# Log-softmax backward on one core: unequal pieces of y, and the next group's first piece queued ahead of each store

## The chip, the cores and the metric

The kernel runs on one NeuronCore of a Trainium2 chip, the other cores idle. The metric is device time in microseconds (us); lower is better. Three runs of the kernel before, taken ahead of everything else, gave a median of 1867.34 us (1867.21 to 1867.37). The span in a profile is about 1.9 us shorter than the time (1865.4 against 1867.34 for the kernel before).

## The reference

```python
batch, seq_len, vocab = 8, 1024, 8192            # float32, 8192 rows of 8192
def reference(y, dy):
    softmax_x = np.exp(y)
    sum_dy = np.sum(dy, axis=-1, keepdims=True)
    return (dy - softmax_x * sum_dy).astype(np.float32)
```

Two tensors of 268.4 MB are read and one of 268.4 MB is written: 805.3 MB in all. The arithmetic needs the row sum of dy, one exponential per element, and one multiply-add per element.

## The kernel before

A group is 256 rows, two neighbouring rows on each of 128 partitions, so a group's dy, y and output are tiles of 128 x 16384 columns; there are 32 groups. dy has two buffers and is overwritten in place by the result. y has two half-size buffers of 8192 columns and is overwritten in place by its exponential.

```python
    R = 2; CD = D // 2
    dyp = ctx.enter_context(tc.tile_pool(name="dyp", bufs=2))
    yp = ctx.enter_context(tc.tile_pool(name="yp", bufs=R))

    def load_dy(g):                       # one transfer, then minus the row sums
        dy_t = dyp.tile([P, R * D], fp32, name="dy_t")
        nc.sync.dma_start(out=dy_t[:], in_=dy_v[g])
        ...                               # nc.vector.tensor_reduce(..., op=ALU.add, negate=True)

    def compute(dy_t, s_t, y_ts):         # four pieces of 4096 columns
        for r in range(R):
            for c in range(0, D, CD):
                e = y_ts[r][:, c : c + CD]
                d = dy_t[:, r * D + c : r * D + c + CD]
                nc.scalar.activation(e, e, EXP)
                nc.vector.scalar_tensor_tensor(out=d, in0=e, scalar=s_t[:, r : r + 1],
                                               in1=d, op0=ALU.mult, op1=ALU.add)
    cur = load_dy(0)
    for g in range(G):
        ...                               # the last two groups are cut here
        y_ts = load_y(g)                  # two transfers of 8192 columns
        compute(*cur, y_ts)
        nxt = load_dy(g + 1)
        store(g, cur[0])
        cur = nxt
```

All transfers are issued from SyncE's queue, in program order: y, y, dy of the next group, store, and again. A transfer that has to wait holds up those behind it. The store waits for the last multiply-add of its group. The dy load waits for the store before it, whose buffer it takes.

Of the kernel before, what the change touches and what calls it, by code (L numbers as in the profile page):

```python
# [1 line left out]

# [5 lines left out]


EXP = mybir.ActivationFunctionType.Exp  # L10
ALU = mybir.AluOpType


@with_exitstack
def kernel(
    ctx: ExitStack,
    tc: tile.TileContext,
    y: bass.AP,
    dy: bass.AP,
    out: bass.AP,  # L20
):



    nc = tc.nc
    P = nc.NUM_PARTITIONS
    fp32 = mybir.dt.float32

    N, D = y.flatten_outer_dims().shape
    R = 2  # L30
    G = N // (P * R)
    assert N == G * P * R
    CD = D // 2

    y_v = y.flatten_outer_dims().rearrange("(g p r) d -> g p (r d)", p=P, r=R)
    dy_v = dy.flatten_outer_dims().rearrange("(g p r) d -> g p (r d)", p=P, r=R)
    out_v = out.flatten_outer_dims().rearrange("(g p r) d -> g p (r d)", p=P, r=R)

    dyp = ctx.enter_context(tc.tile_pool(name="dyp", bufs=2))
    yp = ctx.enter_context(tc.tile_pool(name="yp", bufs=R))  # L40
    stats = ctx.enter_context(tc.tile_pool(name="stats", bufs=2))

    def load_dy(g):
        dy_t = dyp.tile([P, R * D], fp32, name="dy_t")
        nc.sync.dma_start(out=dy_t[:], in_=dy_v[g])
        s_t = stats.tile([P, R], fp32, name="s_t")
        nc.vector.tensor_reduce(  # L47
            out=s_t[:],
            in_=dy_t[:].rearrange("p (r d) -> p r d", r=R),
            axis=mybir.AxisListType.X,  # L50
            op=ALU.add,
            negate=True,
        )
        return dy_t, s_t

    def load_y(g):
        y_ts = []
        for r in range(R):
            y_t = yp.tile([P, D], fp32, name="y_t")
            nc.sync.dma_start(out=y_t[:], in_=y_v[g][:, r * D : (r + 1) * D])  # L60
            y_ts.append(y_t)
        return y_ts

    def compute(dy_t, s_t, y_ts):
        for r in range(R):
            for c in range(0, D, CD):
                e = y_ts[r][:, c : c + CD]
                d = dy_t[:, r * D + c : r * D + c + CD]
                nc.scalar.activation(e, e, EXP)  # L69
                nc.vector.scalar_tensor_tensor(  # L70
                    out=d, in0=e, scalar=s_t[:, r : r + 1], in1=d, op0=ALU.mult, op1=ALU.add
                )

    def store(g, dy_t, parts=1):
        w = R * D // parts
        for k in range(parts):
            nc.sync.dma_start(  # L77
                out=out_v[g][:, k * w : (k + 1) * w], in_=dy_t[:, k * w : (k + 1) * w]
            )

    cur = load_dy(0)
    for g in range(G):
        if g < G - 1:
            y_ts = load_y(g)
            compute(*cur, y_ts)
            nxt = load_dy(g + 1)
            if g < G - 2:
                store(g, cur[0])
                cur = nxt
            else:  # L90
                held, cur = cur, nxt
        else:
            y_ts = load_y(g)
            compute(*cur, y_ts)
            store(g - 1, held[0])
            store(g, cur[0], parts=R)


# [1 line left out]
_INS = ['y', 'dy']  # L100
_OUTS = [((8, 1024, 8192), 'float32')]


# [23 lines left out]
```

## Time and profile before

First the page of the kernel before: busy time by engine (microseconds, share of the span, instructions), the row of the transfer engines in 40 slices (tenths), what they moved in each slice, and the transfer queue (packets, MB, share of 16 engines' span).

```profile
DVE 1119.2 (60%) x160; ACT 457.1 (25%) x129; POOL 0.2 (0%) x4
...
DMA  9999999999999999999999999999999999999999
GB/s 427 416 434 431 443 433 422 435 437 436 427 433 431 440 430 434 431 429 441 433 437 425 433 442 431 434 425 436 438 434 433 428 434 437 437 431 430 429 435 396
...
q1 hardware_dynamic: 18576, 805.31, 99.9%
```

VectorE (DVE) is busy 60%, ScalarE (ACT) 25%, and the 16 transfer engines 99.9%. Moving bytes is the limit. Next is one steady group, near the end of the run, in the timeline of the kernel before (start, duration, engine, line, operation, tile; in brackets the idle time before it and what ended it; SPq is SyncE's queue):

```profile
1741.77 0.34 SPq L77 DMA_DIRECT2D out_dram<-dy_t  x1
1742.21 0.85 SPq L60 DMA_DIRECT2D y_t<-in_y_dram  x2
1748.49 17.22 DVE L47 TENSOR_REDUCE s_t<-dy_t 128x2 f32<-128x16384 f32 x1 [6.75 <-DMA dy_t<-in_dy_dram]
1767.83 0.33 SPq L45 DMA_DIRECT2D dy_t<-in_dy_dram  x1
...
1787.27 7.12 ACT L69 ACTIVATE y_t<-y_t 128x4096 f32<-128x4096 f32 x2 [2.58 <-DMA y_t<-in_y_dram]
```

Read it as a queue. The store is issued at 1741.77. The dy load ahead of it lands at 1748.49, when the reduction that waited for it starts. So 1748.49 - 1741.77 = 6.7 us of work was still queued when the store joined. This is called the reserve at the store here. Likewise the dy load is issued at 1767.83 while y lands until 1787.27: a reserve of 19.4 us. The idea to be tested is that the arithmetic can't cost time as long as no reserve runs out.

The start of the kernel before is tighter:

```profile
22.74 17.22 DVE L47 TENSOR_REDUCE s_t<-dy_t 128x2 f32<-128x16384 f32 x1 [22.74 <-DMA dy_t<-in_dy_dram]
...
57.77 0.35 SPq L77 DMA_DIRECT2D out_dram<-dy_t  x1
58.21 0.92 SPq L60 DMA_DIRECT2D y_t<-in_y_dram  x2
61.83 17.22 DVE L47 TENSOR_REDUCE s_t<-dy_t 128x2 f32<-128x16384 f32 x1 [4.09 <-DMA dy_t<-in_dy_dram]
```

There the reserve is 61.83 - 57.77 = 4.1 us. And the waits of SyncE's queue (total us, times, longest us): SyncE spends its time waiting for the multiply-add (L70) and for stores to land, which is harmless while the engines behind it have work.

```profile
SPq L77 <- DVE dy_t L70: 985.9, 32, 35.0
SPq L45 <- DMA out_dram<-dy_t: 742.0, 30, 25.6
```

| Read from the kernel before | value |
|---|---|
| steady group, reduction start to reduction start | 58.07 us for 25.17 MB, 433.4 GB/s |
| one packet of 65,536 bytes, one of 32,768 bytes (trace records, medians) | 2.418 us, 1.213 us |
| 805.31 MB at 65,536 bytes per 2.418 us on 16 engines (estimate) | 1857 us |

The Trainium skill ("DMA: Bandwidth & Descriptors", "Where 436 GB/s comes from") puts the ceiling of the fabric at 435 GB/s; this trace agrees, with 433.4 GB/s in a steady group.

### The profile page before, as it was taken

The numbers are of one execution on the slowest core, as the hardware profiler recorded it, in microseconds if no ns is written. First come the engines' busy times: TensorE is split into PE (matmuls) and PEld (weight loads), VectorE is DVE, ScalarE is ACT, GpSimd is POOL, SyncE is SP. The second block draws the span as 40 slices with busy tenths as digits, with TensorE's granted clock in tenths as the row PEclk, the third lists the DMA queues.
The fourth block names the chain that finished last, engine by engine and source line by source line (L and its number), as shares of the span: only waits on it lengthen the run. The fifth ranks groups of instructions, "written<-read, shape, count | busy, mean of one in ns | idle before, by whom it ended". The sixth has DMA issues, their size and how long they took to land.

```text
span 1865.4 us, 712 instructions
## 1 busy us (share of the span) xinstructions
DVE 1119.2 (60%) x160; ACT 457.1 (25%) x129; POOL 0.2 (0%) x4
## 2 busy tenths in 40 slices
DVE  5675555755557555575555755657656576565664
ACT  2123321233212332123321233212332113331132
POOL 0000000000000000000000000000000000000000
DMA  9999999999999999999999999999999999999999
GB/s 427 416 434 431 443 433 422 435 437 436 427 433 431 440 430 434 431 429 441 433 437 425 433 442 431 434 425 436 438 434 433 428 434 437 437 431 430 429 435 396
DMA packets 18582, 805.36 MB, mean 432 GB/s; under 512 B 2064, under 2 KB 2064, under 8 KB 2064
## 3 DMA queue, kind: packets, MB, share of 16 engines
q1 hardware_dynamic: 18576, 805.31, 99.9%
q14 instruction: 6, 0.05, 0.0%
HBM read 536.87 MB, written 268.44 MB: 432 GB/s over the span
## 4 chain that ended last, share of the span: by engine, by line
DMA 74%; DVE 17%; ACT 6%; SPq 1%; issue 1%; DVEq 0%; ACTq 0%
DMA y_t<-in_y_dram 69%; DVE dy_t L70 15%; ACT y_t L69 6%; DMA dy_t<-in_dy_dram 3%; DVE s_t L47 2%; DMA out_dram<-dy_t 1%; SPq L60 1%; SPq L77 1%; DVEq L122 0%; ACTq L69 0%; DVEq L70 0%
## 5 line engine op out<-in xcount | busy, mean ns | idle before, releaser
L70 DVE SCALAR_TENSOR_TENSOR dy_t<-y_t,s_t,dy_t 128x4096 f32<-128x4096 f32 x128 | 568.1, 4481 | 490.3 <-ACT y_t L69 490.1
L69 ACT ACTIVATE y_t<-y_t 128x4096 f32<-128x4096 f32 x128 | 455.9, 3608 | 1375.6 <-DMA y_t<-in_y_dram 1375.6
L47 DVE TENSOR_REDUCE s_t<-dy_t 128x2 f32<-128x16384 f32 x32 | 551.0, 17220 | 232.1 <-DMA dy_t<-in_dy_dram 232.1
L69 ACT ACT_TABLE_LOAD x1 | 1.3, 1283 | 0.7 <-PEq L111 0.7
L111 POOL MEMSET const-bfloat16-1.0<- 128x1 bf16 x1 | 0.1, 102 | 0.0
L111 POOL MEMSET const-uint8-127<- 128x1 uint8 x1 | 0.1, 102 | 0.0
L111 POOL MEMSET const-float32-1.0<- 128x1 f32 x1 | 0.1, 99 | 0.0
L111 POOL MEMSET const-float32-0.0<- 128x1 f32 x1 | 0.1, 98 | 0.2 <-issue 0.2
## 6 DMA issues: line engine op xcount, KB each, us to landing
y_t<-in_y_dram SPq DMA_DIRECT2D x64, 4096.0 KB, 35.9
out_dram<-dy_t SPq DMA_DIRECT2D x2, 4096.0 KB, 22.6
dy_t<-in_dy_dram SPq DMA_DIRECT2D x32, 38.7
out_dram<-dy_t SPq DMA_DIRECT2D x31, 26.1
```

The lines of the kernel that those rows point to most:

```text
L47: nc.vector.tensor_reduce(out=s_t[:], in_=dy_t[:].rearrange("p (r d) -> p r d", r=R), axis=mybir.AxisListType.X, op=ALU.add, negate=True,)
L60: nc.sync.dma_start(out=y_t[:], in_=y_v[g][:, r * D : (r + 1) * D])
L69: nc.scalar.activation(e, e, EXP)
L70: nc.vector.scalar_tensor_tensor(out=d, in0=e, scalar=s_t[:, r : r + 1], in1=d, op0=ALU.mult, op1=ALU.add)
L77: nc.sync.dma_start(out=out_v[g][:, k * w : (k + 1) * w], in_=dy_t[:, k * w : (k + 1) * w])
L111: nc = _bacc.Bacc("TRN2", target_bir_lowering=False, num_devices=1)
```

## The change

The intent is to balance the two reserves. y of a group comes as one piece of 5120 and one of 11264 columns. The first piece of the next group goes into the queue ahead of the store, so that more is queued when the store waits for arithmetic; less is then queued when the dy load waits for the store. The arithmetic goes in six pieces, small ones first after the second y piece. The first dy comes by rows, so the first reduction can start sooner. The main lines of the change (left out are, among others, the split first load of dy and a third buffer for the row sums):

```diff
-    CD = D // 2
+    A = 5120
+    A_PIECES = [(0, A)]
+    B_PIECES = [(5120, 6144), (6144, 8192), (8192, 10240), (10240, 13312), (13312, 16384)]
-    yp = ctx.enter_context(tc.tile_pool(name="yp", bufs=R))
+    yap = ctx.enter_context(tc.tile_pool(name="yap", bufs=1))
+    ybp = ctx.enter_context(tc.tile_pool(name="ybp", bufs=1))
...
-    cur = load_dy(0)
-    for g in range(G):
-        ...
+    def first_piece(g, x):
+        compute(*x, load_y(yap, g, 0, A, "ya_t"), 0, A_PIECES)
+    def second_piece(g, x):
+        compute(*x, load_y(ybp, g, A, W, "yb_t"), A, B_PIECES)
+    cur = load_dy(0, split=True)
+    first_piece(0, cur)
+    for g in range(G - 1):
+        second_piece(g, cur)
+        nxt = load_dy(g + 1)
+        first_piece(g + 1, nxt)
+        if g == G - 2:
+            second_piece(g + 1, nxt)
+        nc.sync.dma_start(out=out_v[g], in_=cur[0][:])
+        cur = nxt
+    for c in range(0, W, D):
+        nc.sync.dma_start(out=out_v[G - 1][:, c : c + D], in_=cur[0][:, c : c + D])
```

More of the change, by code (lines that the diff above doesn't have):

```diff
@@ L30 @@
     R = 2
+    W = R * D
     G = N // (P * R)
-    assert N == G * P * R
-    CD = D // 2
+    assert N == G * P * R and D == 8192
+    A = 5120
+    A_PIECES = [(0, A)]
+    B_PIECES = [(5120, 6144), (6144, 8192), (8192, 10240), (10240, 13312), (13312, 16384)]
     y_v = y.flatten_outer_dims().rearrange("(g p r) d -> g p (r d)", p=P, r=R)
@@ L39 @@
     dyp = ctx.enter_context(tc.tile_pool(name="dyp", bufs=2))
-    yp = ctx.enter_context(tc.tile_pool(name="yp", bufs=R))
-    stats = ctx.enter_context(tc.tile_pool(name="stats", bufs=2))
-    def load_dy(g):
-        dy_t = dyp.tile([P, R * D], fp32, name="dy_t")
-        nc.sync.dma_start(out=dy_t[:], in_=dy_v[g])
-        s_t = stats.tile([P, R], fp32, name="s_t")
-        nc.vector.tensor_reduce(
-            out=s_t[:],
-            in_=dy_t[:].rearrange("p (r d) -> p r d", r=R),
-            axis=mybir.AxisListType.X,
-            op=ALU.add,
-            negate=True,
-        )
-        return dy_t, s_t
@@ L56, in load_y @@
-    def load_y(g):
-        y_ts = []
-        for r in range(R):
-            y_t = yp.tile([P, D], fp32, name="y_t")
-            nc.sync.dma_start(out=y_t[:], in_=y_v[g][:, r * D : (r + 1) * D])
-            y_ts.append(y_t)
-        return y_ts
-    def compute(dy_t, s_t, y_ts):
-        for r in range(R):
-            for c in range(0, D, CD):
-                e = y_ts[r][:, c : c + CD]
-                d = dy_t[:, r * D + c : r * D + c + CD]
-                nc.scalar.activation(e, e, EXP)
-                nc.vector.scalar_tensor_tensor(
-                    out=d, in0=e, scalar=s_t[:, r : r + 1], in1=d, op0=ALU.mult, op1=ALU.add
-                )
@@ L74, in store @@
-    def store(g, dy_t, parts=1):
-        w = R * D // parts
-        for k in range(parts):
-            nc.sync.dma_start(
-                out=out_v[g][:, k * w : (k + 1) * w], in_=dy_t[:, k * w : (k + 1) * w]
-            )
-    cur = load_dy(0)
-    for g in range(G):
-        if g < G - 1:
-            y_ts = load_y(g)
-            compute(*cur, y_ts)
-            nxt = load_dy(g + 1)
-            if g < G - 2:
-                store(g, cur[0])
-                cur = nxt
-            else:
-                held, cur = cur, nxt
-        else:
-            y_ts = load_y(g)
-            compute(*cur, y_ts)
-            store(g - 1, held[0])
-            store(g, cur[0], parts=R)
+    yap = ctx.enter_context(tc.tile_pool(name="yap", bufs=1))
@@ new lines, with load_dy @@
+    ybp = ctx.enter_context(tc.tile_pool(name="ybp", bufs=1))
+    stats = ctx.enter_context(tc.tile_pool(name="stats", bufs=3))
+    def load_dy(g, split=False):
+        dy_t = dyp.tile([P, W], fp32, name="dy_t")
+        s_t = stats.tile([P, R], fp32, name="s_t")
+        w = D if split else W
+        for c in range(0, W, w):
+            nc.sync.dma_start(out=dy_t[:, c : c + w], in_=dy_v[g][:, c : c + w])
+        for c in range(0, W, w):
+            nc.vector.tensor_reduce(
+                out=s_t[:, c // D : (c + w) // D],
+                in_=dy_t[:, c : c + w].rearrange("p (r d) -> p r d", d=D),
+                axis=mybir.AxisListType.X,
+                op=ALU.add,
+                negate=True,
+            )
+        return dy_t, s_t
@@ new lines, in load_y, with compute @@
+    def load_y(pool, g, lo, hi, name):
+        y_t = pool.tile([P, hi - lo], fp32, name=name)
+        nc.sync.dma_start(out=y_t[:], in_=y_v[g][:, lo:hi])
+        return y_t
+    def compute(dy_t, s_t, y_t, lo, pieces):
+        for b, e in pieces:
+            y_p, dy_p, r = y_t[:, b - lo : e - lo], dy_t[:, b:e], b // D
+            nc.scalar.activation(y_p, y_p, EXP)
+            nc.vector.scalar_tensor_tensor(
+                out=dy_p, in0=y_p, scalar=s_t[:, r : r + 1], in1=dy_p, op0=ALU.mult, op1=ALU.add
+            )
```

## The prediction

> **What bounds the kernel now.** Moving bytes. Section 1 of the page has VectorE busy 60% and ScalarE 25% of the 1865.4 us span; section 2 has the DMA row at 9 in all 40 slices; section 3 gives the one data queue 99.9% of 16 engines' span for 805.31 MB. In the packet records one 65,536-byte packet takes 2.418 us (27.1 GB/s), 32,768 bytes 1.213 us, back to back on each of 16 engines, so 433.7 GB/s together and 805.31 MB cannot take less than about 1857 us (estimate). The Trainium skill ("DMA: Bandwidth & Descriptors", "Where 436 GB/s comes from") puts the ceiling at 435 GB/s; this trace agrees to 0.4%. The timeline shows a steady group of 58.07 us (last 14 groups, reduction start to reduction start) for 25.17 MB, 433.4 GB/s.
>
> The remaining 7 us: about 2.7 us of start, about 1 us after the last landing, and some 3 us of groups of 58.2 to 58.9 us, nearly all in the first half, where packets ran longer than 2.418 us.
>
> **Does the queue run dry?** Timeline: the store of a group is issued (1741.77) while the dy load ahead of it is still running (it lands by 1748.49): 6.7 us in hand. The dy load is issued (1767.83) with y still landing until 1787.27: 19.4 us in hand. In the first group the store is issued at 57.77, dy lands at 61.83: 4.1 us. No gap appears in the packet records.
>
> **What the change does.** Bytes, tile rows and number of transfers per group (four) stay; one dy load more at the start. Pieces of 20,480 and 45,056 bytes replace two of 32,768: same packet count, same rate. The built order confirms per group: dy, first piece of y, store, second piece, with each store waiting only for its own arithmetic and each dy load for the store before the last.
>
> - In hand at the store's issue: the second piece's arithmetic lasts about 14 us after landing (first exponential 1.1, then about 12.2 us of VectorE at 4.44 us per 4096 columns, with waits between pieces), against dy (19.4) plus first piece (6.0) queued: about 11 us instead of 6.7.
> - In hand at the dy load's issue: the second piece, about 13.3 us instead of 19.4. Still ample.
> - VectorE needs about 36 of 58 us per group, ScalarE about 15: off the path.
> - First dy by rows: the reduction starts about 10 us sooner (near 12), but the first store still waits for the second piece (lands near 42), leaves near 56, and the queue had work until 61.8 anyway.
>
> The change balances a reserve that is already never used up. On the critical path it touches nothing but, at most, the roughly 3 us of uneven groups.
>
> **Prediction.** 1866.5 us, range 1864.0 to 1868.8; faster by over 2%: 0.01, within 2%: 0.98, slower: 0.01.
>
> **What would show it.** Right: DMA row 9 throughout, steady group 58.0 to 58.1 us, packets of 20,480 and 45,056 bytes at the same GB/s, stores issued about 11 us before the first piece lands, first reduction near 12 us, span 1862 to 1867. Wrong: gaps between packets; a steady group away from 58.07.
>
> **What could break it.** Smaller packets slower than in proportion; a buffer or semaphore wait that holds a load until its predecessor is fully done; long packets at the switch between loads and stores becoming more or fewer with the new order, some us either way.

## The result, and the profile after

| | median us | runs |
|---|---|---|
| before | 1867.28 | 6, 1866.88 to 1867.93 |
| after | 1868.12 | 6, 1867.37 to 1868.72 |

The ratio is 1.0004, with a 95% interval of 0.9991 to 1.0017: the same. The page of the changed kernel, the same lines as of before:

```profile
DVE 1130.5 (61%) x225; ACT 463.1 (25%) x193; POOL 0.2 (0%) x4
...
DMA  9999999999999999999999999999999999999999
GB/s 424 416 432 444 424 433 429 435 433 433 433 428 437 427 438 431 436 435 437 427 441 424 442 427 431 434 435 433 435 427 443 429 434 435 424 441 433 430 433 397
...
q1 hardware_dynamic: 18720, 805.31, 99.9%
```

The transfer engines are as full as before. 65 more VectorE instructions cost 11 us of VectorE time in all, off the path. The timeline of the changed kernel, the same group:

```profile
1744.50 0.34 SPq L91 DMA_DIRECT2D out_dram<-dy_t  x1
1744.94 0.38 SPq L66 DMA_DIRECT2D yb_t<-in_y_dram  x1
1749.61 17.22 DVE L55 TENSOR_REDUCE s_t<-dy_t 128x2 f32<-128x16384 f32 x1 [5.14 <-DMA dy_t<-in_dy_dram]
1755.74 4.47 ACT L72 ACTIVATE ya_t<-ya_t 128x5120 f32<-128x5120 f32 x1 [15.46 <-DMA ya_t<-in_y_dram]
...
1774.99 0.33 SPq L53 DMA_DIRECT2D dy_t<-in_dy_dram  x1
...
1788.36 9.96 ACT L72 ACTIVATE yb_t<-yb_t 128x1024 f32<-128x1024 f32 x5 [28.16 <-DMA yb_t<-in_y_dram]
```

When the store joins at 1744.50, the first piece of the next group lands at 1755.74: the reserve at the store is 11.2 us instead of 6.7. When the dy load joins at 1774.99, the second piece lands at 1788.36: 13.4 us instead of 19.4. The change does what it set out to do. The next group's reduction stands at 1807.65, 58.04 us later. The start of the changed kernel:

```profile
12.77 8.69 DVE L55 TENSOR_REDUCE s_t<-dy_t 128x1 f32<-128x8192 f32 x1 [12.77 <-DMA dy_t<-in_dy_dram]
...
56.51 0.35 SPq L91 DMA_DIRECT2D out_dram<-dy_t  x1
...
61.66 17.22 DVE L55 TENSOR_REDUCE s_t<-dy_t 128x2 f32<-128x16384 f32 x1 [5.17 <-DMA dy_t<-in_dy_dram]
```

The first reduction starts 10 us sooner, the first store leaves 1.3 us sooner, and the second dy lands at 61.66 instead of 61.83: bytes decide. SyncE's queue waits as long as before, divided otherwise (in all 1809 us before and 1810 us after; the smaller waits are left out here):

```profile
SPq L53 <- DMA out_dram<-dy_t: 893.9, 30, 30.6
SPq L91 <- DVE dy_t L73: 790.8, 30, 27.0
```

Packets of 20,480 and 45,056 bytes take 762 and 1665 ns (medians), together 2427 ns, as long as two packets of 32,768 bytes (2 x 1213 = 2426).

### The profile page after: what moved, and what is told of

The parts are those of the page before. It is cut to its first block, busy times and chain, and to the rows that moved or that the text cites. A ratio compares the mean times of both kernels' runs of the same rounds, so it can differ in the third digit from the quotient of the medians.

```text
span 1866.5 us, 812 instructions
## 1 busy us (share of the span) xinstructions
DVE 1130.5 (61%) x225; ACT 463.1 (25%) x193; POOL 0.2 (0%) x4
## 3 DMA queue, kind: packets, MB, share of 16 engines
q1 hardware_dynamic: 18720, 805.31, 99.9%
## 4 chain that ended last, share of the span: by engine, by line
DMA 73%; DVE 20%; ACT 5%; SPq 1%; issue 1%; DVEq 0%; ACTq 0%
DMA yb_t<-in_y_dram 70%; DVE dy_t L73 19%; ACT yb_t L72 5%; DMA dy_t<-in_dy_dram 2%; DMA out_dram<-dy_t 2%; DVE s_t L55 1%; SPq L91 1%; DVEq L120 0%; SPq L66 0%; SPq L53 0%; ACTq L72 0%; DVEq L73 0%
## 5 line engine op out<-in xcount | busy, mean ns | idle before, releaser
L73 DVE SCALAR_TENSOR_TENSOR dy_t<-yb_t,s_t,dy_t 128x3072 f32<-128x3072 f32 (+2 forms) x160 | 401.7, 2562 | 533.5 <-ACT yb_t L72 533.5
L55 DVE TENSOR_REDUCE s_t<-dy_t 128x2 f32<-128x16384 f32 (+1 forms) x33 | 551.2, 16703 | 173.9 <-DMA dy_t<-in_dy_dram 173.9
L72 ACT ACTIVATE yb_t<-yb_t 128x3072 f32<-128x3072 f32 (+2 forms) x160 | 318.8, 2067 | 863.8 <-DMA yb_t<-in_y_dram 863.8
L72 ACT ACTIVATE ya_t<-ya_t 128x5120 f32<-128x5120 f32 x32 | 143.0, 4469 | 509.5 <-DMA ya_t<-in_y_dram 509.5
L73 DVE SCALAR_TENSOR_TENSOR dy_t<-ya_t,s_t,dy_t 128x5120 f32<-128x5120 f32 x32 | 177.6, 5551 | 5.0 <-ACT ya_t L72 2.2
```

What stands on the lines that cost most here:

```text
L55: nc.vector.tensor_reduce(out=s_t[:, c // D : (c + w) // D], in_=dy_t[:, c : c + w].rearrange("p (r d) -> p r d", d=D), axis=mybir.AxisLis ...
L72: nc.scalar.activation(y_p, y_p, EXP)
L73: nc.vector.scalar_tensor_tensor(out=dy_p, in0=y_p, scalar=s_t[:, r : r + 1], in1=dy_p, op0=ALU.mult, op1=ALU.add)
```

## The experiments

All ran on 1 core with a profile; times are medians. The "reserve" column is read from each timeline as above, group by group after the first: landing of the last transfer ahead of the store, minus issue of the store. Its range is given where it varies; the low end is the usual one, 11.2 and 6.7 are the steady values. The period is that of groups 1 to 29. A reserve below zero is an overdraft: the last transfer had landed that long before the store was issued.

| kernel | reserve at the store, us | steady period, store to store, median us | time us | ratio to before |
|---|---|---|---|---|
| after | 11.2 | 58.07 | 1868.12 | 1.0004 |
| before | 6.7 | 58.08 | 1867.28 | |
| before + 2048 columns | 5.5 to 6.6 | 58.18 | 1873.90 | 1.0021 |
| after, first piece behind the store | 5.1 to 6.1 | 58.30 | 1874.21 | 1.0026 |
| before + 4096 columns | 3.3 to 4.8 | 58.44 | 1885.46 | 1.01 |
| after + 8192 columns | 2.6 to 3.1 | 58.66 | 1884.42 | 1.0085 |
| after + 12288 columns, ahead | -1.1 to -2.0 | 62.62 | 2006.67 | 1.0731 |
| before + 8192 columns | -1.1 | 61.64 | 1976.91 | 1.0587 |
| first piece behind the store + 8192 columns | -3.5 | 64.32 | 2053.45 | 1.0984 |

(In the last two VectorE itself is busy when dy lands, so the landing is read from the trace's records of each transfer's completion; the usual value is given.)

### More work ahead of the store: does anything use the reserve?

The theory: the queue is never empty, so a later store costs nothing until its reserve is gone, and the changed kernel stands more. The rival: arithmetic already costs, or only bytes can ever matter. The edit puts one more VectorE reduction of N columns, its result thrown away, ahead of the last multiply-add of each group but the last; the output stays right.

```diff
                 nc.scalar.activation(e, e, EXP)
+                if extra and r == R - 1 and c + CD == D:
+                    x_t = stats.tile([P, 1], fp32, name="x_t")
+                    nc.vector.tensor_reduce(
+                        out=x_t[:], in_=dy_t[:, 0:N], axis=mybir.AxisListType.X, op=ALU.add
+                    )
                 nc.vector.scalar_tensor_tensor(
```

> The kernel before, with one more VectorE reduction (128x4096, about 4.3 us by 17.22 us per 16384 columns) ahead of the last arithmetic of every group but the last; its result is thrown away, the output stays right. Theory (the transfer queue is never empty; reserve at the store's issue 6.7 us[...]): 0.4 us of reserve left, so no loss, 1866 to 1869 us. Rival (the store's lateness already costs, part of the time lies in arithmetic): each added us shows, 31 x 4.3 = about 133 us more, 2000 us.

Measured: 1885.46 us, ratio 1.01 (1.0083 to 1.0117). Neither value: not free, and far from the rival's 2000 us. The store still joins ahead of the landing, by 1469.76 - 1466.04 = 3.7 us in this group:

```profile
1466.04 0.34 SPq L82 DMA_DIRECT2D out_dram<-dy_t  x1
...
1469.76 17.22 DVE L47 TENSOR_REDUCE s_t<-dy_t 128x2 f32<-128x16384 f32 x1 [3.74 <-DMA dy_t<-in_dy_dram]
```

So the size of the reserve that is needed was wrong. This expectation and those after it set aside 2 us for it, which no run had shown; what a restart takes is read below, from the queues that did run dry.

> The same with 8192 columns, 8.7 us. Theory: reserve overdrawn by 8.7 + 2.0 - 6.7 = 4.0 us in each of 31 groups, about 124 us more: 1975 to 2010 us, gaps of about 4 us between packets on all engines once a group, steady group about 62 us. Rival (arithmetic costs in full): 31 x 8.7 = 270 us more, 2137 us. Rival (nothing but bytes can matter): 1867 us.

Measured: 1976.91 us (1976.42 to 1977.51), inside the theory's range. Each group now takes about 61.64 us:

```profile
1485.01 17.21 DVE L47 TENSOR_REDUCE s_t<-dy_t 128x2 f32<-128x16384 f32 x1
1485.12 0.34 SPq L82 DMA_DIRECT2D out_dram<-dy_t  x1
...
1546.79 0.34 SPq L82 DMA_DIRECT2D out_dram<-dy_t  x1
```

The sum behind the range holds only in part. The gap between packets is 2.8 us a group and engine instead of 4, and another 0.9 us a group lies in packets that run longer.

> The changed kernel with the same 8.7 us of VectorE work ahead of the last arithmetic piece. Theory (the change raised the reserve at the store to 11.2 us): 11.2 - 8.7 - 2.0 = 0.5 us left, no loss, 1867 to 1870 us, over 5% faster than the kernel before with the same extra work. Rival (the change does nothing at all to the reserve, or the thinner reserve at the dy load takes it back): as slow as the kernel before with it, near 1990 us.

Measured: 1884.42 us, ratio 1.0085. The changed kernel with this extra work is 92 us (4.7%) faster than the kernel before with it, so the larger reserve is real. But it isn't quite free, where no loss was expected. Its timeline shows a reserve of 1535.76 - 1533.09 = 2.7 us:

```profile
1533.09 0.34 SPq L96 DMA_DIRECT2D out_dram<-dy_t  x1
...
1535.76 4.47 ACT L72 ACTIVATE ya_t<-ya_t 128x5120 f32<-128x5120 f32 x1 [15.49 <-DMA ya_t<-in_y_dram]
```

> The changed kernel with 12288 columns, 12.9 us. Theory: overdrawn by 12.9 + 2.0 - 11.2 = 3.7 us in each of 31 groups: about 115 us more, 1965 to 2005 us. Rival (reserve larger than thought, or not what decides): 1868 us.

Measured: 1868.20 us, no loss at all, against the theory's 1965 to 2005. The timeline tells why: the scheduler had put the reduction behind the last multiply-add, so the store did not wait for it.

```profile
1500.41 11.27 DVE L78 SCALAR_TENSOR_TENSOR dy_t<-yb_t,s_t,dy_t 128x2048 f32<-128x2048 f32 x4 [0.52 <-ACT yb_t L72]
1511.60 12.95 DVE L75 TENSOR_REDUCE x_t<-dy_t 128x1 f32<-128x12288 f32 x1
1511.71 0.34 SPq L96 DMA_DIRECT2D out_dram<-dy_t  x1
```

So as a test of the reserve this run missed. It serves as a control instead: 12.95 us more of VectorE work in each of 31 groups, behind the store's condition, cost nothing. The next one repeats the test with a reduction over columns 4096 to 16384, which the last multiply-add overwrites, so that it must come first.

```diff
-                    out=x_t[:], in_=dy_t[:, 0:12288], axis=mybir.AxisListType.X, op=ALU.add
+                    out=x_t[:], in_=dy_t[:, 4096:16384], axis=mybir.AxisListType.X, op=ALU.add
```

> The 12.9 us of d_after_12288 again, which there turned out to stand behind the last arithmetic piece; here the reduction reads columns that the last piece overwrites, so it must come before it. From the two overdrawn runs a group costs the overdraft plus 2.4 to 2.7 us. Theory (reserve of the changed kernel 11.2 us at the store): overdrawn by about 12.9 - 11.2 = 1.7 us, so 4.1 to 4.4 us x 31 = 127 to 136 us more: 1990 to 2010 us. Rival (the place of the work does not matter, VectorE has time enough): 1868 us as in d_after_12288.

```profile
1493.32 12.95 DVE L75 TENSOR_REDUCE x_t<-dy_t 128x1 f32<-128x12288 f32 x1
1506.38 3.42 DVE L78 SCALAR_TENSOR_TENSOR dy_t<-yb_t,s_t,dy_t 128x3072 f32<-128x3072 f32 x1
1508.25 4.47 ACT L72 ACTIVATE ya_t<-ya_t 128x5120 f32<-128x5120 f32 x1 [15.83 <-DMA ya_t<-in_y_dram]
...
1509.83 0.34 SPq L96 DMA_DIRECT2D out_dram<-dy_t  x1
```

Measured: 2006.67 us (2006.66 to 2007.13), inside the theory's range. The first piece has landed before the store is issued: the queue is dry. The same 12.95 us cost 138 us ahead of the last multiply-add and nothing behind it. A group takes 62.62 - 58.07 = 4.55 us longer, of which about 2.0 us is the usual overdraft (1509.83 - 1508.25 = 1.6 us in the group shown); the remaining 2.5 us is what an empty queue costs besides. The packet records divide it: 0.38 us from the end of the last packet to the landing, 0.84 us from the store's issue to its first packet, and most of the rest in packets that run longer (time beyond 2.418 us per 65,536 bytes: 39.3 us per engine in the run instead of 7.1, about 1 us a group). The other two overdrawn runs give 2.5 and 2.7 us in the same way. The Trainium skill ("DMA: Bandwidth & Descriptors", "Anatomy of one DMA — SWDGE (gpsimd) path") gives about 2.0 us of fixed cost, setup and completion, for a transfer issued on another path; the two parts here that compare with it, 0.84 + 0.38 = 1.2 us, are smaller.

### One part undone: the first piece behind the store

```diff
         nxt = load_dy(g + 1)
-        first_piece(g + 1, nxt)
         if g == G - 2:
+            first_piece(g + 1, nxt)
             second_piece(g + 1, nxt)
         nc.sync.dma_start(out=out_v[g], in_=cur[0][:])
+        if g < G - 2:
+            first_piece(g + 1, nxt)
```

> The changed kernel with one thing undone: the next group's first piece is queued behind the store, not ahead of it. Theory: reserve at the store falls to 19.4 - 14.3 = about 5 us, still above the 2 us needed: 1866 to 1869 us, the same. Rival (queueing ahead is worth something today): slower than the changed kernel by some us to 1%.

Measured: 1874.21 us (1873.98 to 1874.61), ratio 1.0026 (1.0011 to 1.0042) to the kernel before. The reserve is what was expected, but it isn't free; the number that came true is the rival's, some us of loss:

```profile
1516.12 0.34 SPq L91 DMA_DIRECT2D out_dram<-dy_t  x1
...
1521.21 17.22 DVE L55 TENSOR_REDUCE s_t<-dy_t 128x2 f32<-128x16384 f32 x1 [5.11 <-DMA dy_t<-in_dy_dram]
```

> The same with the 8.7 us reduction ahead of the last arithmetic piece. Theory (the place of the first piece alone makes the reserve): overdrawn by 8.7 + 2.0 - 5.1 = 5.6 us x 31 = about 174 us: 2010 to 2065 us, where the changed kernel with the same work stays near 1868. Rival (the six pieces or the first dy by rows make the changed kernel tolerant): near 1868 us.

Measured: 2053.45 us (2052.58 to 2053.92), inside the theory's range, and 169 us slower than the changed kernel with the same work (on another chip). So it is the place of the first piece that makes the larger reserve; the six pieces and the first dy by rows, which stayed, do not make it. Equal pieces with the first queued ahead of the store were not run, so what the unequal cut adds is not shown.

> The kernel before with 2048 columns, 2.2 us, of which about 0.8 us fills a wait for the exponential: reserve at the store about 5.3 us. Theory now (the 16 engines stand up to 3.4 us apart, so about 3.4 + 2 = 5.4 us of reserve are needed before the first one runs short): just at the edge, 1867 to 1873 us, like the kernel with the first piece behind the store, whose reserve is 5.1 us (1874 us). Rival (that kernel's 6 us come from its pieces or its order, not from the reserve): 1867 us, no loss.

Measured: 1873.90 us (1872.76 to 1875.20), ratio 1.0021 (1.0005 to 1.0037). That is 0.9 us above the theory's range of 1867 to 1873, and nearer to it than to the rival's 1867. The kernel before, brought to about the same reserve by other means, loses about the same few us as the kernel with its first piece behind the store, which speaks for the reserve and against the pieces as the cause of that loss. A caution: on this chip 5 of 11 runs of the kernel before itself took 1871.0 to 1875.4 us, the others 1867.4 to 1868.3; the interval is only just clear of 1. The traces agree with the reading: time in long packets (explained below) is 11.4 us per engine here and 12.2 us there, against 6.1 in the kernel before.

### All arithmetic taken out

```diff
     def compute(dy_t, s_t, y_ts):
-        for r in range(R):
-            ...
+        pass
```

The reduction in the dy load goes too. The loads and stores stay, in order; the output is dy as it came, wrong. (The comparison with the reference let it pass: exp(y) is 1/8192 on average and a sum of 8192 draws of size 1 is about 90, so the missing term is some 0.01.)

> The kernel before with all arithmetic taken out: the same loads and stores in the same order, the store sends dy as it came (a wrong result on purpose). Theory (the engines that move bytes set the time, no wait for arithmetic ever empties their queue): 1865 to 1868 us, the same as with arithmetic. Rival (the first half's uneven groups, about 3 us, or more, are waits for arithmetic): 1858 to 1864 us.

> The changed kernel with all arithmetic taken out in the same way (a wrong result on purpose). Theory: 1865 to 1869 us, the same as the floor of the kernel before, because bytes, packets and their rate are the same. Rival (the change gained by its larger reserve and gave it back by dearer pieces): this floor is some us above the floor of the kernel before, which then is below the kernel before.

Measured: 1867.71 us (1867.11 to 1868.14) and 1867.69 us (1867.36 to 1868.95); ratios to before 0.9991 (0.9979 to 1.0004) and 0.9993 (0.998 to 1.0005). The page of the kernel before without arithmetic:

```profile
DMA  9999999999999999999999999999999999999999
...
q1 hardware_dynamic: 18576, 805.31, 99.9%
```

Both floors are alike, and both kernels stand on them (the changed kernel's 1868.12 us is from another chip). No store waits for arithmetic there, and the reserve at the store is about 38 us in both; it buys no time. All the arithmetic of the kernel costs nothing that these runs can tell, and the changed pieces are no dearer. One thing is left: on this chip 9 runs of the kernel before took 1867.2 to 1872.7 us, 4 of them over 1869.5, while all 10 floor runs stayed at or below 1869.0. The kernel before may lose some us there, its reserve of 6.7 us being near the edge. The changed kernel was not run on that chip, so whether it would be steadier there is open.

### Where the last 3 us go: uneven groups

Both kernels have groups longer than 58.07 us, nearly all in the first third; the changed kernel has one of 58.86 later, from group 20 to 21. These are the differences of the reductions' starts in the kernel before and in the changed kernel, from group 1 to 2 on:

```
before 58.50 58.12 58.43 58.41 58.28 58.88 58.05 58.19 58.07 58.16 57.99 58.06 58.38 58.06 58.08 58.07 ...
after  58.60 58.15 58.39 58.49 58.22 58.94 58.21 58.24 58.61 58.25 57.93 58.05 58.06 58.09 58.06 58.06 ...
```

The trace records each packet, and for each transfer the 16 engines' finish. From these, two sums by engine: time in packets longer than their bytes at 2.418 us per 65,536, and the span between the first and the last engine's finish of a transfer.

| kernel | long packets, us per engine | first to last finish in group 0, 5, 10, 20, us |
|---|---|---|
| before | 6.1 | 0.7, 1.9, 3.0, 3.4 |
| after | 7.1 | 0.5, 1.1, 2.5, 2.6 |
| before, no arithmetic | 6.1 | 0.8, 2.4, 2.6, 3.2 |
| before, groups reversed | 5.7 | 0.7, 2.0, 2.5, 2.7 |
| after, first piece behind the store | 12.2 | 0.5, 1.2, 2.5, 3.3 |
| before + 4096 columns | 19.5 | 0.5, 0.8, 1.1, 1.9 |
| after + 8192 columns | 24.3 | 0.3, 0.7, 0.7, 0.6 |

The engines start in step and drift about 3.4 us apart, and the long packets of the undisturbed kernels fall in the groups in which they drift. Even the late group of 58.86 us in the changed kernel is the one in which this spread jumps, from 2.7 to 3.5 us. Does the spread explain the size of the reserve needed? The first engine is done 3.4 us ahead of the last, a landing follows the last packet by 0.4 us, and a first packet follows its issue by 0.84 us: about 4.6 us must be queued for no engine to run short (an estimate from these figures). But time is already lost at 5.1 to 6.6 us, and in longer packets, so the spread is not the whole account. Two runs were to test whether it is the being in step that makes packets long.

> The kernel before with the groups taken in reverse order (last rows first). Theory (the uneven groups come from the engines' starting in step): uneven groups again in the first third of the run, 1866 to 1869 us. Rival (they belong to certain rows of the tensors): they move to the last third.

```diff
-        nc.sync.dma_start(out=dy_t[:], in_=dy_v[g])
+        nc.sync.dma_start(out=dy_t[:], in_=dy_v[G - 1 - g])      # y and out alike
```

Measured: 1867.78 us (1866.42 to 1869.54). The reductions start 58.61, 58.41, 58.37, 58.26, 58.05, 58.29, 58.41 us apart, and then 58.07: uneven in the first third again. So they do not belong to certain rows of the tensors. With arithmetic gone they stay too, so they aren't waits for it.

> The kernel before with one reduction of 12288 columns (12.9 us), in group 16 only, ahead of its last arithmetic (it reads columns that this overwrites, so it must come first). The queue runs dry once, by about 12.9 - 6.7 + 2.5 = 8.7 us. Theory (uneven groups come when the 16 engines are in step, as at the start, and end when they have drifted 3 us apart): after group 16 the spread of the engines' finish falls from 3.4 to under 1 us and the next 5 to 10 groups are uneven again (58.2 to 58.6 us), although the reserve is back at 6.7 us: about 1877 to 1880 us. Rival (only a late store itself makes packets long): the groups after it are 58.07 us at once, about 1876 us.

```diff
-            compute(*cur, y_ts)
+            compute(*cur, y_ts, extra=g == 16)     # the reduction of columns 4096 to 16384
```

Measured: 1870.46 us (2 runs), against 1876 to 1880 expected by either. The run missed its aim. In this group the scheduler moved the first y load of the next group ahead of the late store, by itself:

```profile
977.58 0.33 SPq L60 DMA_DIRECT2D y_t<-in_y_dram  x1
...
1000.47 0.34 SPq L82 DMA_DIRECT2D out_dram<-dy_t  x1
...
1003.78 7.12 ACT L69 ACTIVATE y_t<-y_t 128x4096 f32<-128x4096 f32 x2 [21.93 <-DMA y_t<-in_y_dram]
```

The store joined with 3.3 us still queued, so the queue as a whole never ran dry, and the engines were pulled from 3.6 to 1.4 us of each other, not to under 1; within two groups they stood 3.2 us apart again. It is the change's own device, seen once: a store 13 us late cost 2.9 us in the trace (the two dy landings behind it came 60.09 and 58.93 us apart instead of 58.07). In the time itself, 1870.46 us, that can't be told from the spread of the kernel before on this chip. Whether being in step makes packets long therefore stays open.

In the kernels with a reserve between 2.6 and 5.5 us the loss lies in long packets and hardly in idle engines: with 4096 columns the long packets rise from 6.1 to 19.5 us per engine, idle time (from the run's first packet to its last) only from 2.6 to 5.7; with 8192 columns after the change, long packets rise from 7.1 to 24.3 and idle time from 2.7 to 3.3. It is not VectorE's extra work as such: with 12288 columns behind the store's condition, long packets sum to 6.4 us. In the steady groups most of the long packets begin 16 to 26 us after the store's issue, at the end of the store and the start of the loads behind it. Why a store that joins late makes these packets longer is not known from these runs.

## Why the prediction was right

- **Bytes bound the kernel.** Shown: without any arithmetic the same transfers take 1867.71 us, and 99.9% stays 99.9%.
- **The change balances a reserve that is never used up.** Shown, with the sizes given: 11.2 us at the store (predicted about 11), 13.4 us at the dy load (about 13.3), first reduction at 12.77 (near 12), first store at 56.51 (near 56). The steady groups stayed at 58.03 to 58.11, but for the one of 58.86.
- **The smaller packets cost the same.** Shown: 762 + 1665 = 2427 ns against 2 x 1213 = 2426 ns, and the two floors agree within their runs.
- **At most the 3 us of uneven groups is touched.** It held: before, the 30 intervals from group 1 to group 31 are 1744.75 - 30 x 58.07 = 2.7 us above an even pace, after 1745.99 - 30 x 58.07 = 3.9 us. That 1.2 us is the profiled spans' difference (1865.4 and 1866.5), and it is within the noise of the runs. The prediction leaned to 0.8 us faster, the median came 0.8 us slower; neither is clear of noise.
- **What the prediction took too lightly.** It took 6.7 us for a reserve that is never used up without saying how much is needed. The experiments' first expectation, 2 us, fell: from about 5.5 us down, time is lost, at first 0.1 to 0.6 us a group. The kernel before stands just above that edge, so the change was worth nothing on the first chip, but for a smaller reason than the prediction's wording suggests.

No version that was run beats both. The bytes alone take about 1857 us (estimate from the packet's 2.418 us), and the transfers without arithmetic already take what both kernels take.

## What to carry to other kernels

In a kernel bound by transfers, read the reserve: when a transfer that waits for arithmetic joins the queue, how many us are still queued ahead of it? If it is comfortably above the edge below which time is lost (here between about 5.5 and 6.7 us, and on two chips perhaps a little higher), moving work around it is worth nothing, however sensible; if the arithmetic per group is about to grow, the same change is worth a great deal (92 us with 8.7 us more per group). And look at where the scheduler put an added instruction before reading its time: the same 12.95 us cost 138 us ahead of the store's condition and nothing behind it.

## What the Trainium skill lacked or had wrong

- "DMA: Bandwidth & Descriptors", "Where 436 GB/s comes from", says that for transfers between HBM and SBUF the HBM side (about 358 GB/s, half of what two cores share) binds, though the same paragraph notes a measured 425 GB/s. This core, alone, moved 433.4 GB/s in a steady group, reads and writes mixed. "HBM Reference", "Specifications (TRN2)", has it better: a core streaming alone is bounded by its 16 DMA engines (about 425 GB/s there).
- No page says how much must stay queued for the 16 engines to lose nothing. Here 6.7 us was enough on the first chip, 5.1 to 5.6 us, as a rule, lost about 0.25% and 2.7 us 0.85%, mostly in packets that ran longer, not in idle engines.
- No page says how far apart the engines of one transfer finish, here 0.7 us at first and about 3.4 us later, nor that groups are uneven (58.1 to 58.9 us for 58.07) while they do.
- "DMA: Bandwidth & Descriptors" has no time per packet for transfers issued from SyncE. Here it was in proportion to bytes from 20,480 to 65,536 within 1%: 762, 1213, 1665 and 2418 ns.
